# Second layer's u and z weights: the unrounded rest made by an adding transfer in place of a VectorE subtraction

## Chip, core and metric

The kernel runs on one core of one Trainium2 chip. The time is that of one execution on the device in microseconds; what is compared is the median of several executions. The core has five engines that work side by side, each through its own queue of instructions in order: TensorE (PE, the matmuls, with PEld for the loading of weights), VectorE (DVE), ScalarE (ACT), GpSimd (POOL) and SyncE (SP, which issues transfers). Sixteen DMA engines carry the transfers that these queues issue.

## What is computed

A trunk of two layers is applied to 512 prompt tokens and to 8 samples of 4 tokens (544 tokens in all), with a width of 1024. The first layer is an RWKV-7 mixer, the second a gated MLP over chunks of 128 tokens. The change lies in the second:

```python
def _gmlp_mixer(h, w_in, v_g, v_b, ws, bs, w_out):
    proj = h @ w_in                       # 1024 -> 3 x 2048
    u = jax.nn.gelu(proj[..., :e])
    v = jax.nn.gelu(proj[..., e:2 * e])
    z = proj[..., 2 * e:]
    ...                                   # v is normalised
    mixed = jnp.einsum('gts,bcsgd->bctgd', wm, vp) + bs.T[None, None, :, :, None]
    ...
    o = u * mixed * jax.nn.silu(z)
    return o @ w_out, v
```

All inputs and outputs are float32.

## The kernel before

**Precision.** PE multiplies in a rounded float32 format (float32r in the code). To keep the product close to float32, each operand is split in two: a rounded part (`hi`) and the rest that rounding dropped (`lo` = raw - hi). One product then takes three matmuls: `mm3` (L218 to L221) runs hi weights with hi activations (L219), hi weights with lo activations (L220), and lo weights with hi activations (L221), in this order. So every block of weights needs two further steps between its load and its use.

**Weights.** `load` (L117) takes a slot of the tag "raw" and has SP issue the transfer of a block from memory: 128 partitions x 1024 values, 512 KB. `halves` (L122) rounds it on ACT into a slot of "whi" (L125) and has DVE subtract the rounded from the raw block into a slot of "wlo" (L126). `weights` (L129) does one after the other. Each of the three tags has two slots, shared by all weights of the kernel: a block takes the slot of the block before last, and may write to it only when that one's last reader is done.

**The second layer's loop** (L1401 to L1429) goes over f = 0 to 15, 128 columns of u and z at a time. In each turn `project` (L230) is called for u (L1409; the names in the profile are gu_r for the raw block, gu_h and gu_l for its parts, gu_p for the result) and for z (L1425; gz_r, gz_h, gz_l, gz_p). A call makes the two parts of the weights, then runs two halves of 272 tokens of 8 x 3 matmuls each, 48 in all, and evacuates each half from the result bank: DVE multiplies by the norm's factor (L1406, L1420) and ACT takes the Gelu (L1407) or the Tanh (L1422). Between the two calls stands `mix(f - 1)` for f > 0 (L1376): ten small matmuls (L1382, L1383), then DVE and ACT form the gated output of the block and split it (goh, gol). Results rotate over five PSUM banks (`bank`, L225).

After f = 4, 8 and 12, `out_project` (L238) multiplies four finished blocks by the output weights: eight small blocks of weights (go_r, go_h, go_l; 256 KB each) with 24 matmuls each (go__p), which take their slots from the same three tags, and DVE adds the results to the residual xT (L247). At f = 12 the residual is also transposed (L1446, pfy; L1452 and L1453 for the samples, with two copies on POOL). In the tail behind the loop (L1455 to L1558) the last four blocks are multiplied out, added and normed.

In this loop nobody writes the order of the instructions by hand. A planner takes the program and lays out each engine's queue ahead of time, by the order of the program and by its own estimates of when operands and slots are ready; it also places all semaphores. The queues are then fixed, and each engine runs its own in order. (The first layer's order is written out by hand; it isn't touched. Nor are the v weights of the second layer or its output weights, which keep `halves`.)

Of the kernel before, what the change touches and what calls it, by code (L numbers as in the profile page):

```python
# [7 lines left out]
F32R = mybir.dt.float32r  # L8
ALU = mybir.AluOpType
AF = mybir.ActivationFunctionType  # L10
# [5 lines left out]
KD = 8  # L16
# [58 lines left out]
def build(tc, A, O, off):  # L75
    nc = tc.nc
    V, S, G, T, Q = nc.vector, nc.scalar, nc.gpsimd, nc.tensor, nc.sync
# [3 lines left out]
    with ctx:  # L81
        cp = ctx.enter_context(tc.tile_pool(name="cp", bufs=1))
        wp = ctx.enter_context(tc.tile_pool(name="wp", bufs=3))
# [33 lines left out]
        def load(name, src, nk, w=128, q=Q):  # L117
            raw = wp.tile([128, 1024 // w, w], F32, name=name + "_r", tag="raw", bufs=2)
            q.dma_start(raw[:, 0:nk, :], src)
            return name, raw, nk, w  # L120

        def halves(name, raw, nk, w=128):  # L122
            hi = wp.tile([128, 1024 // w, w], F32R, name=name + "_h", tag="whi", bufs=2)
            lo = wp.tile([128, 1024 // w, w], F32R, name=name + "_l", tag="wlo", bufs=2)
            S.activation(hi[:, 0:nk, :], raw[:, 0:nk, :], AF.Copy)  # L125
            V.tensor_tensor(out=lo[:, 0:nk, :], in0=raw[:, 0:nk, :], in1=hi[:, 0:nk, :], op=ALU.subtract)  # L126
            return hi, lo

        def weights(name, src, nk, w=128):  # L129
            return halves(*load(name, src, nk, w))  # L130
# [6 lines left out]
        with tc.tile_pool(name="st", bufs=1) as st:  # L137
# [46 lines left out]
            for h in range(2):  # L184
                for k in range(KD):
                    ks = slice(128 * k, 128 * k + 128)
                    pool, tag = banks[(8 * h + k) % 6]
# [30 lines left out]
        def mm3(ps, whi, wlo, ahi, alo, first, last):  # L218
            T.matmul(ps, whi, ahi, start=first, stop=False)  # L219
            T.matmul(ps, whi, alo, start=False, stop=False)  # L220
            T.matmul(ps, wlo, ahi, start=False, stop=last)  # L221
# [3 lines left out]
        def bank(name):  # L225
            pool, tag = ((ppp, "pp"), (ppp, "pp"), (p1, "g"), (p1, "s"), (p1, "y"))[turn_[0] % 5]
            turn_[0] += 1
            return pool.tile([128, 512], F32, name=name, tag=tag)

        def project(name, w, evac):  # L230
            hi, lo = weights(name, w, KD)
            for h in range(2):
                ps = bank(name + "_p")[:, 0:HT]
                for k in range(KD):
                    mm3(ps, hi[:, k, :], lo[:, k, :], hh[:, k, h, :], hl[:, k, h, :], k == 0, k == KD - 1)
                evac(h, ps)
# [997 lines left out]
        with tc.tile_pool(name="l1", bufs=1) as l1, tc.tile_pool(name="l1t", bufs=2) as lt:  # L1234
# [166 lines left out]
            for f in range(NF):  # L1401
                gu = lt.tile([128, 2, HT], F32, name=f"gu{f}", tag="gu", bufs=2)

                def uevac(h, ps, f=f, gu=gu):
                    a = lt.tile([128, HT], F32, name=f"ua{f}", tag="va")
                    V.tensor_tensor(out=a, in0=ps, in1=bc[:, h, :], op=ALU.mult)  # L1406
                    S.activation(gu[:, h, :], a, AF.Gelu_apprx_tanh)  # L1407

                project(f"gu{f}", A["g_u"][f], uevac)  # L1409
                if f % 4 == 0:  # L1410
                    normalise(f // 4)
# [6 lines left out]
                def z1evac(h, ps, f=f, gz=gz):  # L1418
# [4 lines left out]
                    V.scalar_tensor_tensor(out=gz[:, h, :], in0=th, scalar=1.0, in1=a, op0=ALU.add, op1=ALU.mult)  # L1423

                project(f"gz{f}", A["g_z"][f], z1evac)  # L1425
                V.scalar_tensor_tensor(out=gz, in0=gu, scalar=0.5, in1=gz, op0=ALU.mult, op1=ALU.mult)
                if f in (4, 8, 12):
# [40 lines left out]
            for q in range(4):  # L1468
                if q < 2:
                    hi, lo = (wp.tile([128, 4, 256], F32R, name=f"gl{q}_{n}", tag=f"w{n}", bufs=2) for n in ("hi", "lo"))  # L1470
                else:
                    hi, lo = (x[:, :, 256 * q - 512 : 256 * q - 256] for x in (hv, lv))
                raw = ws[:, :, 256 * q : 256 * q + 256]
# [137 lines left out]
```

## Time and profile before

| | |
|---|---|
| time, median of 3 runs | 1267.81 us (1265.22 to 1268.55) |
| the profiled execution's own time | 1269.8 us |
| its span, first to last instruction | 1268.0 us |
| mean granted TensorE clock | 0.998 |
| the u and z loop in the span | from 948.5 to about 1241 us |
| the same: u matmuls (gu_p), per line L219, L220, L221 | 256 each |
| loads gu_r and gz_r | 16 each, 512 KB, issued by SP |

The profile is of one execution. A row of a group reads: line, engine, operation, output<-input, partitions x elements, count | busy us in all, mean ns of one | us for which the engine stood idle just before them, and what ended that idle time. In a timeline a row begins with its start (us from the start of the span) and its duration. Matmuls overlap in the pipeline, so the starts of two that follow each other are closer (0.12 to 0.13 us) than the duration shown (0.29 us). SPq marks the issue of a transfer by SP.

### The profile page before, as it was taken

The page shows a single profiled execution, that of the slowest core. Times are in us where ns is not written, and L with a number is a line of the kernel's source. Part 1 is how long each engine was busy: PE and PEld are TensorE (multiplying, and loading weights), DVE is VectorE, ACT ScalarE, POOL GpSimd, SP SyncE. Part 2 cuts the span into 40 slices and gives each one's busy share as a digit, 9 for nine tenths or more (in the row PEclk, how much of TensorE's full clock was granted, in tenths as well). Part 3 has the DMA queues.
Part 4 walks back from the last instruction along what each step waited for, and adds up shares of the span by engine and source line. Part 5 has one row for each costly group of instructions (what it writes and reads, how often), then busy time and mean ns, then how long its engine had stood idle before and what let it go on. Part 6 is the DMA issues. An engine that isn't in the chain of part 4 may idle for free.

```text
span 1268.0 us, 34549 instructions
## 1 busy us (share of the span) xinstructions
PE 1229.7 (97%) x14432; PEld 1154.6 (91%) x14432; DVE 949.8 (75%) x2205; ACT 663.0 (52%) x1523; POOL 132.4 (10%) x346
## 2 busy tenths in 40 slices
PE   6999999999999999999998999999999999999997
PEld 5899999999999999999997889987779999999997
DVE  5789999999999999998987866573248656656466
ACT  5677567657666775676665552243243323232343
POOL 1212021111102120211211100100000000000000
PEclk9999999999999999999999999999999999999999
DMA  5322432332333234224232363432222232231511
GB/s 179 100 73 82 112 88 76 103 94 73 91 103 92 64 86 119 66 77 116 68 89 71 106 193 113 140 98 70 98 94 77 64 110 79 78 103 58 164 37 71
DMA packets 113508, 119.74 MB, mean 94 GB/s; under 512 B 77992, under 2 KB 81448, under 8 KB 113352
## 3 DMA queue, kind: packets, MB, share of 16 engines
q1 hardware_dynamic: 113352, 117.54, 30.8%
q8 instruction: 113, 1.85, 0.6%
q14 instruction: 43, 0.35, 0.1%
HBM read 99.79 MB, written 17.72 MB: 93 GB/s over the span
## 4 chain that ended last, share of the span: by engine, by line
PE 85%; DVE 6%; DMA 4%; ACT 3%; issue 1%; POOL 1%; SPq 1%; POOLq 0%; DVEq 0%; ACTq 0%
PE r_p L219 3%; PE gz_p L219 3%; PE v_p L219 3%; PE gu_p L219 3%; PE gz_p L220 3%; PE gz_p L221 3%; PE gu_p L221 3%; PE gu_p L220 3%; PE k_p L219 2%; PE r_p L221 2%; PE r_p L220 2%; PE gv_p L1317 2%; PE pgo L547 2%; PE v_p L221 2%; PE v_p L220 2%; PE gv_p L1318 2%
## 5 line engine op out<-in xcount | busy, mean ns | idle before, releaser
L219 PE MATMUL v_p<-hh,v_h 128*128 128x272 f32 x256 | 78.6, 307 | 0.9 <-ACT raw L362 0.9
L219 PE MATMUL r_p<-hh,r_h 128*128 128x272 f32 x256 | 78.8, 308 | 0.0
L219 PE MATMUL k_p<-hh,k_h 128*128 128x272 f32 x256 | 78.3, 306 | 0.0
L219 PE MATMUL z_p<-hh,z_h 128*128 128x272 f32 x256 | 77.7, 304 | 0.0
L219 PE MATMUL gz_p<-hh,gz_h 128*128 128x272 f32 x256 | 75.2, 294 | 0.0
L221 PE MATMUL r_p<-hh,r_l 128*128 128x272 f32 x256 | 74.2, 290 | 0.0
L219 PE MATMUL gu_p<-hh,gu_h 128*128 128x272 f32 x256 | 74.2, 290 | 0.0
L220 PE MATMUL r_p<-hl,r_h 128*128 128x272 f32 x256 | 74.1, 289 | 0.0
L221 PE MATMUL gu_p<-hh,gu_l 128*128 128x272 f32 x256 | 73.9, 289 | 0.0
L220 PE MATMUL gu_p<-hl,gu_h 128*128 128x272 f32 x256 | 73.9, 289 | 0.0
L221 PE MATMUL z_p<-hh,z_l 128*128 128x272 f32 x256 | 73.8, 288 | 0.0
L221 PE MATMUL gz_p<-hh,gz_l 128*128 128x272 f32 x256 | 73.8, 288 | 0.0
L221 PE MATMUL k_p<-hh,k_l 128*128 128x272 f32 x256 | 73.8, 288 | 0.0
L221 PE MATMUL v_p<-hh,v_l 128*128 128x272 f32 x256 | 73.8, 288 | 0.0
L220 PE MATMUL gz_p<-hl,gz_h 128*128 128x272 f32 x256 | 73.7, 288 | 0.0
L220 PE MATMUL k_p<-hl,k_h 128*128 128x272 f32 x256 | 73.7, 288 | 0.0
L220 PE MATMUL v_p<-hl,v_h 128*128 128x272 f32 x256 | 73.6, 288 | 0.0
L220 PE MATMUL z_p<-hl,z_h 128*128 128x272 f32 x256 | 73.6, 287 | 0.0
L221 PE MATMUL go__p<-goh,go_l 128*128 128x272 f32 x192 | 55.5, 289 | 0.0
L219 PE MATMUL go__p<-goh,go_h 128*128 128x272 f32 x192 | 55.3, 288 | 0.0
L220 PE MATMUL go__p<-gol,go_h 128*128 128x272 f32 x192 | 55.1, 287 | 0.0
L364 POOL COPY shl<-raw 128x9 f32<-128x9 f32 x49 | 11.0, 225 | 409.6 <-ACT raw L362 409.4
(415 smaller groups left out, 4487.9 us busy)
## 6 DMA issues: line engine op xcount, KB each, us to landing
k_r<-w_in SPq DMA_DIRECT2D x16, 512.0 KB
r_r<-w_in SPq DMA_DIRECT2D x16, 512.0 KB
v_r<-w_in SPq DMA_DIRECT2D x16, 512.0 KB
z_r<-w_in SPq DMA_DIRECT2D x16, 512.0 KB
gu_r<-g_u SPq DMA_DIRECT2D x16, 512.0 KB
gz_r<-g_z SPq DMA_DIRECT2D x16, 512.0 KB
go_r<-g_out SPq DMA_DIRECT2D x24, 256.0 KB
od<-of SPq DMA_DIRECT2D x16, 272.0 KB
```

What stands on the lines that cost most here:

```text
L219: T.matmul(ps, whi, ahi, start=first, stop=False)
L220: T.matmul(ps, whi, alo, start=False, stop=False)
L221: T.matmul(ps, wlo, ahi, start=False, stop=last)
L364: G.tensor_copy(shl[:, :, f], raw[:, 512:553:5])
L547: T.matmul(pg[h][:, 128 * j : 128 * j + 128], BK[rs, c].rearrange("p a b -> p (a b)"), AR[rs, :, c, :], start=True, stop=True)
L1317: T.matmul(ps[i], ah, hi, start=k == 0, stop=False)
L1318: T.matmul(ps[i], al, hi, start=False, stop=False)
```

## The change

`project` no longer calls `weights`. It loads the raw block as before and rounds it on ACT as before. The lo tile is then first filled with the negated rounded block, by a second pass on ACT (a copy with scale -1). After that POOL issues a transfer that reads the same block of weights from memory a second time and adds it, in the DMA engines, onto what stands in the tile: lo = -hi + w. The subtraction on DVE goes away, for the 32 blocks of u and z. `halves`, `out_project`, the v weights and the first layer stay.

```diff
         def project(name, w, evac):
-            hi, lo = weights(name, w, KD)
+            _, raw, nk, _ = load(name, w, KD)
+            hi = wp.tile([128, KD, 128], F32R, name=name + "_h", tag="whi", bufs=2)
+            lo = wp.tile([128, KD, 128], F32R, name=name + "_l", tag="wlo", bufs=2)
+            S.activation(hi, raw, AF.Copy)
+            S.activation(lo, hi, AF.Copy, scale=-1.0)
+            G.dma_start(lo, w, accum_op=ALU.add)
             for h in range(2):
                 ps = bank(name + "_p")[:, 0:HT]
                 for k in range(KD):
```

## The prediction

> **What bounds the kernel now.** I read the page's busy shares first, then its DMA queues, then the busy time by stretches for the second layer's u and z loop (from the first u matmul at 948.5 to the last z matmul, about 1241) and for the tail behind it.
>
> ```profile
> PE 1229.7 (97%) x14432; PEld 1154.6 (91%) x14432; DVE 949.8 (75%) x2205; ACT 663.0 (52%) x1523; POOL 132.4 (10%) x346
> ...
> q1 hardware_dynamic: 113352, 117.54, 30.8%
> q8 instruction: 113, 1.85, 0.6%
> q14 instruction: 43, 0.35, 0.1%
> ...
> 948.50:1241.00 292.50, 292.44 (x2346) 291.55 (x2347) 185.65 (x372) 91.73 (x152) 2.01 (x4) 1.00 0.27 86
> 1241.00:1268.00 27.00, 20.35 (x188) 19.07 (x186) 14.99 (x45) 11.13 (x40) 2.73 (x5) 0.95 0.21 83
> ```
>
> The columns of the stretches are PE, PEld, DVE, ACT and POOL busy, then granted clock, DMA share and GB/s. In the loop PE is busy 292.44 of 292.50 us at full clock; DVE has 107 us to spare, ACT 201, POOL almost everything. So the loop is a row of matmuls with nothing between them, and whatever VectorE is spared there can give back at most 0.06 us. The change can only cost, unless it reaches the 6.65 us without PE in the tail, where no u or z weight is made. No queue of POOL's appears among the DMA queues: what the change adds has no row of its own in this trace.
>
> Next I looked at how early the weights are ready, in groups by line and shape (count, busy us, mean ns, idle before and its releaser).
>
> ```profile
> L126 DVE TENSOR_TENSOR gz_l<-gz_r,gz_h 128x1024 fp32r<-128x1024 f32 x16 | 19.6, 1225 | 11.1 <-ACT gz_h L125 11.0
> L126 DVE TENSOR_TENSOR gu_l<-gu_r,gu_h 128x1024 fp32r<-128x1024 f32 x16 | 19.5, 1216 | 4.6 <-ACT gu_h L125 4.6
> L125 ACT ACTIVATE gz_h<-gz_r 128x1024 fp32r<-128x1024 f32 x16 | 17.0, 1061 | 32.5 <-PE gz_p L220 21.9 <-PE go__p L220 5.9 <-DMA gz_r<-g_z 4.8
> L125 ACT ACTIVATE gu_h<-gu_r 128x1024 fp32r<-128x1024 f32 x16 | 16.9, 1057 | 28.4 <-PE gu_p L220 18.0 <-PE go__p L220 7.1 <-DMA gu_r<-g_u 3.2
> ```
>
> The rounding on ACT is mostly released by PE (gu_p, gz_p, go__p L220): with two slots for rounded weights, block n+1 can be rounded only when PE has finished block n-1, that is while block n runs. The weights themselves have long landed. So what counts is the time from the end of block n-1 to the first matmul of block n+1 that reads the rest (L221).
>
> **The change part by part.** Removed: 32 subtractions on DVE, 19.6 + 19.5 = 39.1 us. DVE isn't the bound, so this gives nothing by itself, and what becomes late in its place is the new chain. Added on ACT: 32 negations of the same shape as the rounding, 1.06 us each, about 34 us on an engine with 201 us free. A Gelu or Tanh behind one waits up to 1.06 us longer; it is hidden by the block of 48 matmuls (about 6 us, from 954.66 to 960.81 in the rows below) that PE runs meanwhile, since the result banks rotate by five. Added on POOL: 32 transfers of 512 KB, which wait there for the negation. Behind them in POOL's queue stand only the next transfers and, after the last output block, two small copies for PE's transposes. SP's loads are freed earlier:
>
> ```profile
> SPq L119 <- DVE gu_l L126: 71.7, 12, 7.7
> ```
>
> This is the loads' own wait for the subtraction; it now ends with the rounding. That gains nothing, as ACT waited for loads for only 3.2 + 4.8 us in all, at the start of the loop.
>
> The path that can set the end is rounding, negation, transfer, first L221. Call X the time from the end of the negation to the matmul being free to go. Four places have different room for X.
>
> ```profile
> 1000.23 1.06 ACT L125 ACTIVATE gz_h<-gz_r 128x1024 fp32r<-128x1024 f32 x1 [1.99 <-PE gz_p L220]
> 1007.50 0.29 PE L221 MATMUL gz_p<-hh,gz_l 128*128 128x272 f32 x1
> ...
> 954.66 1.06 ACT L125 ACTIVATE gu_h<-gu_r 128x1024 fp32r<-128x1024 f32 x1
> 960.81 0.29 PE L221 MATMUL gu_p<-hh,gu_l 128*128 128x272 f32 x1
> ...
> 1034.44 1.06 ACT L125 ACTIVATE gu_h<-gu_r 128x1024 fp32r<-128x1024 f32 x1 [2.38 <-PE go__p L220]
> 1037.63 0.29 PE L221 MATMUL gu_p<-hh,gu_l 128*128 128x272 f32 x1
> ...
> 1188.07 1.06 ACT L125 ACTIVATE gu_h<-gu_r 128x1024 fp32r<-128x1024 f32 x1 [2.38 <-PE go__p L220]
> 1192.48 0.28 PE L221 MATMUL gu_p<-hh,gu_l 128*128 128x272 f32 x1
> ```
>
> These are rows in order of time (start, duration). After two ACT passes (2.12 us) the room is:
> - in the steady pattern 1007.50 - 1000.23 - 2.12 = 5.15 us. If block gu(f) is late by d, gz(f) behind it gains that d, so a late chain costs X - 5.15 once in each f, not twice. It holds for f = 2, 3, 4, 6, 7, 8, 10, 11, 12, 14, 15: 11 times.
> - at gu1, where no mix stands between gu0 and gz0: 960.81 - 954.66 - 2.12 = 4.03 us, once.
> - at gu5 and gu9, behind the output projection whose blocks last only some 3 us: 1037.63 - 1034.44 - 2.12 = 1.07 us, twice. Today's subtraction needs 1.2 us there from the end of the rounding and just fits.
> - at gu13: 1192.48 - 1188.07 - 2.12 = 2.29 us; the transposes pfy that stand among its matmuls could be moved ahead by the planner, which I don't count on.
>
> So the cost is 11(X - 5.15) + (X - 4.03) + 2(X - 1.07) + (X - 2.29), each bracket only where positive; above 5.15 it is 15X - 65.1.
>
> Now X, bounded by rows.
>
> ```profile
> 935.70 0.33 SPq L119 DMA_DIRECT2D gu_r<-g_u  x1
> 939.08 1.06 ACT L125 ACTIVATE gu_h<-gu_r 128x1024 fp32r<-128x1024 f32 x1 [3.15 <-DMA gu_r<-g_u]
> ...
> 1037.50:1040.00 2.50, 2.50 (x22) 2.50 (x21) 1.66 (x2) 1.02 (x1) 0.00 (x0) 1.00 0.61 210
> ...
> 951.51 1.19 POOL L1353 TENSOR_TENSOR rl<-rl,nhalf 128x5 f32<-128x5 f32 x1
> ...
> DMA packets 1028, 0.06 MB, mean 65 GB/s; under 512 B 1028, under 2 KB 1028, under 8 KB 1028
> ...
> 371.00:372.00 1.00, 1.00 (x10) 1.00 (x10) 0.93 (x4) 0.64 (x2) 0.00 (x0) 1.00 0.64 65
> ```
>
> A plain load of 512 KB on SP's queue took 939.08 - 935.70 = 3.38 us from issue to the rounding that waited for it: the low end, as the new transfer moves these bytes too. Its data kept all 16 DMA engines busy for 2.5 x 0.61 = 1.5 us (the second stretch holds one such load, 210 GB/s x 2.5 us = 0.52 MB). Adding must also read the target, so I take the data twice: +1.5 us. POOL issues it in place of SP; for its setup I take the dearest POOL instruction of the stage, 1.2 us, though it may be nothing. X = 3.4 + 1.5 + 1.2 = 6.1 us. The far end is a transfer cut into small pieces: the stretch 371 to 372 moved 0.065 MB in 0.64 us of all engines, so 2 x 0.52 MB would need 10.3 us, and X = 3.4 - 1.5 + 10.3 + 1.2 = 13.4 us. I take 6.1, nearest to the load's own rows, since the tile is laid out as in that load.
>
> Sum at X = 6.1: 15 x 6.1 - 65.1 = 26.4 us (10.5 steady, 2.1 at gu1, 10.1 at gu5 and gu9, 3.8 at gu13). Memory traffic doesn't add to this: 32 x 3 us in 292 us lifts the DMA share from 0.27 to about 0.6. The profiled execution took 1269.8 us, of which 1268.0 are its span; it becomes 1296.2. The median shown is 1267.8, 2.0 below, so I forecast 1294.
>
> The Trainium skill, DMA: Bandwidth & Descriptors, section "Anatomy of one DMA", gives a POOL-issued transfer as 2.0 us plus bytes over 436 GB/s; for 512 KB this is an estimate of 3.2 us, by which the sum would be 5.2 us and the time 1273. No run here shows a POOL transfer; the plain load above, at 3.38 us, lies close. Against the change speaks SBUF — State Buffer, section "Who interferes with whom" of the Trainium skill: while VectorE runs in a mode that takes both ports, POOL cannot write its descriptors.
>
> ```profile
> L1358 DVE TENSOR_SCALAR Vt<-Vt,mv,rl 128x512 f32<-128x512 f32 x16 | 8.0, 531 | 1.7 <-POOL rl L1353 1.7
> ```
>
> This is the loop's candidate, at 1.04 ns per column against 1.19 for the subtractions above. That isn't the halving such a mode would show, so by this trace the lock should add nothing; held up by one such instruction, a transfer would lose at most 0.53 us.
>
> **The rivals.**
> - Light transfer: X between 3.4 and 5.15, setup hidden or the target read alongside. Steady blocks don't wait; the places behind the output projection do: 5.8 us at 3.4, 12.1 at 5.15, so 1274 to 1280. For it: the load's 3.38 us. Against: the extra read. Chance 0.27. The formula of the Trainium skill falls here.
> - Heavy transfer: X from 7.5 to 13.4, because adding is slower than reading, or POOL prepares slowly. 47 to 136 us, so 1315 to 1404. For it: small packets do run at 65 GB/s here. Against: whole rows of 4 KB are contiguous. Chance 0.24.
> - Not slower (the other side): the planner orders everything in this loop anew. If it lets gu5, gu9 and gu13 be rounded one output block (3 us) earlier, their room grows to 4.1 to 5.3 us, and with X below 4.03 no place waits: 1268. For it: it already mixes gu13 with the transposes. Against: slots are given out in the order of the program, and PE's idle 0.06 us leaves nothing to win. Chance 0.06.
> - It doesn't do what it says: a rounded target may make the transfer go element by element. At 0.64 x 16 / 1028 = 10 ns a packet, 2 x 131072 elements on 16 engines need 164 us per transfer, and the loop becomes milliseconds. Chance 0.05.
>
> **How the numbers follow.** The forecast case, X from 5.15 to 7.5 (1280 to 1315), has 0.38. The range must leave out no more than 2 in 10: I drop the element-wise case, most of the not-slower case, and the heavy one above X = 10 (15 x 10 - 65.1 = 85 us, 1353), about 0.09. That gives 1272 to 1353. A measurement of this kernel can tell about 0.3% (3.8 us) from no change. Even the lightest transfer costs 5.8 us, so "within" is nearly all of the not-slower case: faster 0.02, same 0.05, slower 0.93.
>
> **What would show it.** POOL's queue with 32 issues; PE idle before gu_p L221 and gz_p L221, put down to a transfer. X read as the gap from the end of a negation to that matmul; PE waits of about X - 1.07 at gu5 and gu9, and of X - 5.15 once in each steady f. DVE 39 us lighter, ACT 34 us heavier. The forecast is wrong if steady blocks don't wait (X under 5.15), if both blocks of each f wait (then the slots aren't what links them), or if ACT's rounding starts late for another reason.

## The result and the profile after

| | before | after |
|---|---|---|
| median (lowest to highest) of 4 runs each | 1268.18 us (1265.22 to 1273.35) | 1305.8 us (1299.48 to 1311.6) |
| the profiled execution, its span | 1269.8, 1268.0 us | 1311.6, 1309.8 us |

The changed kernel takes 1.0291 times as long, with an interval of 1.0261 to 1.0321: 37.6 us more, where 26 were forecast. The profile is of one of the longer executions, 41.8 us longer in its span, and that is the number to be explained.

First the page of after: busy time by engine, and two of the DMA queues (packets, MB, share of 16 engines).

```profile
PE 1242.3 (95%) x14432; PEld 1165.4 (89%) x14432; DVE 917.0 (70%) x2173; ACT 693.3 (53%) x1555; POOL 160.6 (12%) x378
...
q1 hardware_dynamic: 113352, 117.54, 29.8%
q0 software_dynamic: 4608, 16.78, 7.7%
```

The work moved as the diff says. DVE lost 32 instructions and 32.8 us, ACT gained 32 and 30.3 us, POOL gained 32 and 28.2 us, and a queue that wasn't there before carries 16.78 MB, which is 32 blocks of 512 KB. (Busy time counts overlapping records once; the durations of the instructions that went and came add up to 39.1 us on DVE and 33.5 on ACT.) PE has the same 14432 matmuls but is busy 12.6 us longer. So the same matmuls took it longer, and that was no part of the forecast.

The busy time by stretches, the loop and then the tail (columns as in the prediction):

```profile
948.10:1282.70 334.60, 306.51 (x2350) 302.60 (x2347) 154.49 (x342) 120.53 (x183) 28.21 (x34) 0.96 0.53 122
1282.70:1309.80 27.10, 20.40 (x188) 19.13 (x187) 15.04 (x45) 11.13 (x40) 2.75 (x5) 0.97 0.21 83
```

All of it is in the loop: 334.6 us where it was 292.5, while the tail kept its 27 us. PE now stands idle for 334.60 - 306.51 = 28.1 us there and is busy for 306.51 - 292.44 = 14.1 us more (over the whole kernel it is 12.6, since outside the loop PE's busy time also differs between the two executions), and its granted clock is 0.96 where it was 1.00. The list of PE's waits (us in total, times, longest) names the releaser:

```profile
PE gu_p L221 <- DMA gu_l<-g_u: 26.8, 14, 3.5
...
PE gz_p L221 <- DMA gz_l<-g_z: 1.3, 2, 1.0
```

These two rows make 28.1 us. So 41.8 = 28.1 of waiting for the adding transfers + 12.6 by which PE is busy longer + about 1 elsewhere.

One chain, at f = 6, in the timeline of after (start, duration, engine, and in brackets the idle time before it):

```profile
1059.48 1.06 ACT L234 ACTIVATE gu_h<-gu_r 128x1024 fp32r<-128x1024 f32 x1 [1.75 <-PE gu_p L220]
1060.77 1.05 ACT L235 ACTIVATE gu_l<-gu_h 128x1024 fp32r<-128x1024 f32 x1
1062.11 0.86 POOL L236 DMA_DIRECT2D gu_l<-g_u  x1 [10.25 <-ACT gu_l L235]
...
1065.20 0.29 PE L219 MATMUL gu_p<-hh,gu_h 128*128 128x272 f32 x1
1067.48 0.39 PE L221 MATMUL gu_p<-hh,gu_l 128*128 128x272 f32 x1 [2.00 <-DMA gu_l<-g_u]
```

It is the chain that the prediction drew: PE's last use of an old slot releases the rounding, then come negation, POOL's issue, the landing, and the first L221. X, from the end of the negation (1061.82) to L221, is 5.66 us here. The matmul before L221 started at 1065.20, and matmuls follow each other by 0.125 us, so PE was ready for L221 at 1065.33. The room was 3.5 us, and PE stood idle for about the rest.

### The profile page after: what moved, and what is told of

The parts are those of the page before. It is cut to its first block, busy times and chain, and to the rows that moved or that the text cites. A ratio compares the mean times of both kernels' runs of the same rounds, so it can differ in the third digit from the quotient of the medians.

```text
span 1309.8 us, 34637 instructions
## 1 busy us (share of the span) xinstructions
PE 1242.3 (95%) x14432; PEld 1165.4 (89%) x14432; DVE 917.0 (70%) x2173; ACT 693.3 (53%) x1555; POOL 160.6 (12%) x378
## 3 DMA queue, kind: packets, MB, share of 16 engines
q0 software_dynamic: 4608, 16.78, 7.7%
## 5 line engine op out<-in xcount | busy, mean ns | idle before, releaser
L221 PE MATMUL gu_p<-hh,gu_l 128*128 128x272 f32 x256 | 79.0, 311 | 26.8 <-DMA gu_l<-g_u 26.8
L221 PEld LDWEIGHTS gu_p<-hh,gu_l 128*128 128x128 f32 x256 | 52.2, 205 | 29.8 <-DMA gu_l<-g_u 29.8
L219 PE MATMUL gu_p<-hh,gu_h 128*128 128x272 f32 x256 | 78.0, 306 | 0.0
L220 PE MATMUL gu_p<-hl,gu_h 128*128 128x272 f32 x256 | 77.8, 304 | 0.0
L1411 DVE TENSOR_TENSOR ua<-gu_p,bc 128x272 f32<-128x272 f32 x32 | 14.1, 441 | 90.1 <-PE gu_p L221 90.1
L221 PE MATMUL gz_p<-hh,gz_l 128*128 128x272 f32 x256 | 73.7, 289 | 1.3 <-DMA gz_l<-g_z 1.3
L221 PE MATMUL r_p<-hh,r_l 128*128 128x272 f32 x256 | 74.4, 291 | 0.0
L220 PE MATMUL r_p<-hl,r_h 128*128 128x272 f32 x256 | 74.4, 291 | 0.0
L221 PE MATMUL z_p<-hh,z_l 128*128 128x272 f32 x256 | 73.9, 288 | 0.0
L221 PE MATMUL k_p<-hh,k_l 128*128 128x272 f32 x256 | 73.8, 288 | 0.0
L221 PE MATMUL v_p<-hh,v_l 128*128 128x272 f32 x256 | 73.7, 288 | 0.0
L220 PE MATMUL k_p<-hl,k_h 128*128 128x272 f32 x256 | 73.7, 288 | 0.0
L220 PE MATMUL v_p<-hl,v_h 128*128 128x272 f32 x256 | 73.7, 288 | 0.0
L220 PE MATMUL gz_p<-hl,gz_h 128*128 128x272 f32 x256 | 73.6, 288 | 0.0
L220 PE MATMUL z_p<-hl,z_h 128*128 128x272 f32 x256 | 73.6, 287 | 0.0
L953 POOL TENSOR_TENSOR m<-m,nhalf 128x9 f32<-128x9 f32 x16 | 34.3, 2144 | 177.9 <-DVE m L951 177.9
```

The lines of the kernel that those rows point to most:

```text
L953: G.tensor_tensor(out=m2, in0=m2, in1=nhalf[:, 0:9], op=ALU.pow)
```

## The experiments

Two theories stood against each other. **Theory A**, of the prediction: a block costs what its chain (rounding, negation, transfer) lacks in room before the first L221, so a late chain is paid once per f and goes away with room. **Rival B**: the 32 transfers, ACT passes or POOL issues cost by themselves (traffic, queues, contention), so each costs its share wherever its result is used. Then it had to be found out where the 12.6 us of PE's busy time came from. Each ratio is against the kernel before on the same chip; its medians there were 1267.15 us (19 runs) for `u_only`, `z_only`, `idle_transfers` and `rest_last`, 1269.73 (11) for `third_slot`, `neg_first`, `plain` and `warm`, and 1269.13 (14) for `rest_later_2`, `halves` and `again`.

**Only the u blocks, only the z blocks.** `u_only` and `z_only` use the new chain for one of the two and the old subtraction for the other (the diff is that of `u_only`; `z_only` asks for "gz"):

```diff
-            _, raw, nk, _ = load(name, w, KD)
...
+            if name.startswith("gu"):
+                _, raw, nk, _ = load(name, w, KD)
...
+                G.dma_start(lo, w, accum_op=ALU.add)
+            else:
+                hi, lo = weights(name, w, KD)
```

> The new chain for the u weights alone; z keeps VectorE's subtraction. Theory A (a late chain costs PE once in each f, since a wait at gu gives gz its room; long waits then halve the granted clock for some us): nearly the whole loss stays, 1298 to 1308 us against 1268 before and 1306 with both; PE waits before gu_p L221 of about 27 us. Rival B (each of the 32 transfers costs its own share of the 38 us): half, 1287 us.

Measured: 1299.58 us, ratio 1.0259 (1.0221 to 1.0297), within A's range.

> The new chain for the z weights alone; u keeps VectorE's subtraction. Theory A: the steady blocks wait once in each f, now before gz_p L221, some 1.5 us in 12 turns, but not behind the output projection, where gz has 3 us more room: 15 to 20 us of waits and a little clock, 1283 to 1293 us; so the two halves together lose clearly more than the whole. Rival B: the halves add up to the whole, with u_only at 1287 this one at 1287.

Measured: 1301.53 us, ratio 1.0271 (1.0233 to 1.031), longer than either theory gave. The list of PE's waits in `u_only` has for the loop:

```profile
PE gu_p L221 <- DMA gu_l<-g_u: 22.8, 15, 3.6
```

And that of `z_only`:

```profile
PE gz_p L221 <- DMA gz_l<-g_z: 19.2, 15, 2.6
```

The changed kernel keeps its 26.8 us of u waits nearly whole when the z blocks are taken out of the change (22.8), and its two z waits become 15 when the u blocks are. Either half costs 32 to 34 us; both together cost 38, not 67. A price per transfer is ruled out by that; that it is paid once per f stands. What made `z_only` longer than expected isn't the waiting (19.2 us, where theory A had 15 to 20) but PE's busy time, 1243.3 us, 13.6 above before, 11.0 of it in the loop (297.81 us from the first u to the last z matmul, 286.83 before). Theory A had allowed for only "a little clock" there.

**The transfers without a waiter.** `idle_transfers` is the kernel before plus, for each block, a transfer of 512 KB that adds onto a spare tile which nobody reads, released by the rounding:

```diff
             hi, lo = weights(name, w, KD)
+            G.tensor_copy(sc[:, 0, 0:1], hi[:, 0, 0:1])
+            G.dma_start(sc, w, accum_op=ALU.add)
```

> The kernel before, VectorE's subtraction kept, and beside it 32 adding transfers of the same blocks into a spare tile that nobody reads, each released by the rounding of its block through a copy of one column on POOL. Theory A: 1267 to 1271 us, no PE waits. Rival C: if the transfers' traffic or POOL's issues disturb the others, 1280 us or more.

Measured: 1269.05 us, ratio 1.0011 (0.9994 to 1.0028). Its loop:

```profile
948.50:1241.00 292.50, 292.44 (x2356) 291.35 (x2349) 185.73 (x373) 92.16 (x153) 40.60 (x66) 1.00 0.59 142
```

PE is busy 292.44 of 292.50 us, exactly as before, though the DMA share went from 0.27 to 0.59. Traffic and POOL's queue cost nothing; B falls for these.

**The same chain, used later.** `rest_last` keeps the whole change (32 negations, 32 adding transfers) and only turns the order of the 48 matmuls: those on `hi` of both halves first, the 16 on the rest last. That puts 32 matmuls between the start of a block and its first use of `lo`.

```diff
+            pss = [bank(name + "_p")[:, 0:HT] for _ in range(2)]
             for h in range(2):
-                ps = bank(name + "_p")[:, 0:HT]
                 for k in range(KD):
-                    mm3(ps, hi[:, k, :], lo[:, k, :], hh[:, k, h, :], hl[:, k, h, :], k == 0, k == KD - 1)
-                evac(h, ps)
+                    T.matmul(pss[h], hi[:, k, :], hh[:, k, h, :], start=k == 0, stop=False)
+                    T.matmul(pss[h], hi[:, k, :], hl[:, k, h, :], start=False, stop=False)
+            for h in range(2):
+                for k in range(KD):
+                    T.matmul(pss[h], lo[:, k, :], hh[:, k, h, :], start=False, stop=k == KD - 1)
+                evac(h, pss[h])
```

> The change as it is, but PE runs the 32 matmuls of a block that read the rounded weights first, for both halves, and the 16 that read the rest last: the need for the rest moves 4 us later, and the rounding comes out of its chain. All transfers and both passes on ACT stay. Theory A: room grows from 5.15 to some 10 us, and to some 6 behind the output projection; PE waits nearly vanish, granted clock 1.00, 1268 to 1273 us. Rival C (the loss comes from the transfers' traffic, from ACT's 34 us or from POOL): no cover helps, 1290 us or more.

Measured: 1269.19 us, ratio 1.0011 (0.9988 to 1.0035). Its engines on the page:

```profile
PE 1227.0 (97%) x14432; PEld 1153.0 (91%) x14432; DVE 916.4 (72%) x2173; ACT 695.7 (55%) x1555; POOL 159.8 (13%) x378
```

And its loop among the stretches:

```profile
948.50:1241.00 292.50, 289.67 (x2328) 288.54 (x2327) 151.27 (x334) 122.02 (x179) 27.84 (x33) 1.00 0.58 138
```

DVE, ACT and POOL show the changed kernel's work, yet PE is idle for 2.8 us instead of 28.1 (two waits, at gu5 and gu9), the clock is back at 1.00, and no difference from before can be told. The ACT passes are excluded with that too. The 37 us are the price of waiting in the wrong place, with what a wait costs PE besides, and not of the work itself.

**In between.** `rest_later_2` does the same within each half: 16 matmuls on `hi`, then 8 on `lo`.

```diff
                 for k in range(KD):
-                    mm3(ps, hi[:, k, :], lo[:, k, :], hh[:, k, h, :], hl[:, k, h, :], k == 0, k == KD - 1)
+                    T.matmul(ps, hi[:, k, :], hh[:, k, h, :], start=k == 0, stop=False)
+                    T.matmul(ps, hi[:, k, :], hl[:, k, h, :], start=False, stop=False)
+                for k in range(KD):
+                    T.matmul(ps, lo[:, k, :], hh[:, k, h, :], start=False, stop=k == KD - 1)
```

> The change with the matmuls on the rest moved last within each half of a block: the first need comes 2 us later (16 matmuls), half of the move in rest_last, and the rounding's slot comes free 1 us before the block's end. Theory A: room for the transfer grows from 5.15 to some 8 us, steady waits vanish; gu1, gu5, gu9 and gu13 keep up to 2 us each: 1270 to 1278 us, PE waits under 8 us. If the cover were not what counts, about 1300.

Measured: 1276.42 us, ratio 1.0075 (1.0046 to 1.0105). Its waits:

```profile
PE gu_p L243 <- DMA gu_l<-g_u: 5.3, 2, 3.0
```

Two waits are left, at gu5 and gu9 behind the output projection (3.0 and 2.3 us); all others are covered. Behind the first the clock was halved for 3.4 us, behind the second it wasn't, as the stretches behind the two show:

```profile
1041.10:1044.40 3.30, 3.30 (x17) 3.30 (x16) 0.44 (x1) 0.43 (x1) 0.00 (x0) 0.50 0.92 202
1121.40:1124.40 3.00, 3.00 (x24) 3.00 (x25) 0.44 (x1) 0.83 (x2) 0.00 (x0) 1.00 1.01 209
```

**An earlier start by a third slot.** In `third_slot` every third block has a `lo` tile of its own, so that the chain of a block needn't wait for the block before last. For this the tile is filled ahead of `hi`, with the negated raw block; the write rounds it as it rounds `hi`, so the sum is the same.

```diff
-                lo = wp.tile([128, KD, 128], F32R, name=name + "_l", tag="wlo", bufs=2)
-            S.activation(hi, raw, AF.Copy)
-            S.activation(lo, hi, AF.Copy, scale=-1.0)
+            if n % 3 == 2:
+                lo = uzp.tile([128, KD, 128], F32R, name=name + "_l", tag="uzl", bufs=1)
+            else:
+                lo = wp.tile([128, KD, 128], F32R, name=name + "_l", tag="wlo", bufs=2)
+            S.activation(lo, raw, AF.Copy, scale=-1.0)
             G.dma_start(lo, w, accum_op=ALU.add)
+            S.activation(hi, raw, AF.Copy)
```

> A third slot for the rest (every third block of u and z takes it), and the negation made straight from the raw block, so that negation and transfer of block n+1 can start one block earlier. The same bytes, passes and transfers. Theory A (the loss is the chain from the end of block n-1): room grows by about 6 us, no waits but perhaps behind the output projection, 1268 to 1272 us. If the chain's start isn't what counts (the transfer is late for another reason), it stays at 1290 us or more.

Measured: 1285.97 us, ratio 1.0134 (1.0106 to 1.0162): more than half of the loss is gone, but far more is left than was expected. Its waits in the loop:

```profile
PE gu_p L221 <- DMA gu_l<-g_u: 9.8, 3, 3.8
...
PE gu_p L219 <- ACT Vt L1332: 1.8, 1, 1.8
```

Every steady wait is gone, as A has it. The three left are at gu5, gu9 and gu13. There the slot is held by the blocks of the output projection, or, at gu13, the chain waits for the raw block itself (the row of ACT there):

```profile
1201.44 1.06 ACT L237 ACTIVATE gu_l<-gu_r 128x1024 fp32r<-128x1024 f32 x1 [2.05 <-DMA gu_r<-g_u]
```

The expectation had only a "perhaps" for these places: gu5 and gu9 get no third slot of their own (their n, 10 and 18, leaves the remainders 1 and 0), and at gu13, which has it, the raw block comes late. Moving the first pass also cost 1.8 us at the start of the loop, where ACT's v blocks (Vt) now come later, and PE was busy 7.0 us longer.

**The negation first, the rest a little later.** `neg_first` fills `lo` before `hi` is made (as the last one, without the extra tile), and moves the last L220 of a half behind its last L221.

```diff
-            S.activation(hi, raw, AF.Copy)
-            S.activation(lo, hi, AF.Copy, scale=-1.0)
+            S.activation(lo, raw, AF.Copy, scale=-1.0)
             G.dma_start(lo, w, accum_op=ALU.add)
+            S.activation(hi, raw, AF.Copy)
...
+                T.matmul(ps, hi[:, KD - 1, :], hl[:, KD - 1, h, :], start=False, stop=True)
```

> The negation made from the raw block ahead of the rounding, and the last of the matmuls on the rest moved ahead of the last on the rounded weights, so that its slot comes free first. The chain loses one pass on ACT, 1.06 + 0.23 us; bytes and transfers stay. Theory A: 11 steady waits and most of the halved clock go, 1276 to 1288 us. Rival (the transfer's end is set by the memory traffic, not by its start): within 5 us of 1306.

Measured: 1296.21 us, ratio 1.0206 (1.0178 to 1.0234), above the expected range. Its waits:

```profile
PE gu_p L243 <- DMA gu_l<-g_u: 13.7, 8, 3.2
...
PE gu_p L240 <- ACT Vt L1333: 2.1, 1, 2.1
```

The steady waits fell to at most 0.9 us each, as a chain that starts one ACT pass earlier should give. But gu1, gu5, gu9 and gu13 kept 2.8 to 3.2 us each (at the last three the planner still put the rounding first), there were 2.1 us at the start of the loop, and PE was busy 7.1 us longer. Only the steady places had been counted.

**The adding alone.** `plain` writes the tile with a transfer of the same size that doesn't add.

```diff
-            G.dma_start(lo, w, accum_op=ALU.add)
+            G.dma_start(lo, w)
```

> The transfer on POOL without adding: it overwrites the negated block, so the output lacks the subtraction of the rounded part. Theory A: a packet of 4 KB takes 159 ns as in a plain load in place of 328, the transfer is shorter by 8 x 0.17 = 1.35 us; steady waits nearly vanish, gu1, gu5, gu9 and gu13 still wait 1 to 2.5 us: 1273 to 1284 us. Rival (adding costs nothing, POOL's path does): no change from 1300 to 1306 us.

Measured: 1284.29 us, ratio 1.0133 (1.01 to 1.0167), just above its range. POOL's issues (duration in ns: least, median, most) and the time from issue to landing, in the view of the tile gu_l of after:

```profile
L236 POOL DMA_DIRECT2D gu_l<-g_u x16: 860/862/1172, 941.3 to 1258.5; - x16
...
DMA to landing us min/median/max: 5.3/5.7/7.7
```

The same view of `plain`:

```profile
L236 POOL DMA_DIRECT2D gu_l<-g_u x16: 527/528/1170, 940.2 to 1229.9; - x16
...
DMA to landing us min/median/max: 3.7/4.5/5.5
```

Adding lengthens the landing by 1.2 us at the median, of which 0.33 us are POOL's issue. The PE waits fell to 11.8 us and PE was busy 1230.7 us. Even the plain transfer from POOL took 4.5 us, more than the 3.38 us of the plain load on SP from issue to its reader. The Trainium skill, DMA: Bandwidth & Descriptors, section "Anatomy of one DMA", with its 2.0 us plus bytes over 436 GB/s (3.2 us here, an estimate), is too short for both.

**Two smaller transfers.** `halves` cuts the transfer in two of 256 KB each.

```diff
-            G.dma_start(lo, w, accum_op=ALU.add)
+            for b in range(2):
+                G.dma_start(lo[:, 4 * b : 4 * b + 4], w[:, 4 * b : 4 * b + 4], accum_op=ALU.add)
```

> The change with the transfer in two of 256 KB (columns k 0 to 3, then 4 to 7), both issued by POOL one behind the other; the first matmul on the rest waits for the first alone. If a transfer's time is mostly its bytes, the first lands some 1.4 us earlier, steady waits nearly vanish, 1284 to 1294 us. If it is mostly a fixed part (issue, start, landing), little changes, 1297 to 1304 us.

Measured: 1296.98 us, ratio 1.0212 (1.0174 to 1.025), at the border between the two. POOL's issues of gu_l:

```profile
L237 POOL DMA_DIRECT2D gu_l<-g_u x32: 856/1120/1242, 942.2 to 1243.8; - x32
```

Half the bytes don't have a shorter issue (0.86 us at the least, 1.12 at the median, against 0.86 for the whole). At the eight blocks where PE waited for the first half, that came 4.6 to 5.8 us after the end of the negation, 5.1 at the mean, where the whole block takes 6.3 in after: half the bytes are worth some 1.2 us, near the 1.4 of the first theory. But the second half lands about 2 us behind the first, so that PE waits twice in four blocks (gu1, gu5, gu9 and gu10), and PE is busy 1239.0 us. By that some 3.9 of the 6.3 us don't go with the bytes (an estimate); what they consist of wasn't tried.

**Does the slow clock follow the waits?** `warm` gives PE 16 matmuls more, whose results are overwritten, at the head of nine blocks that wait (gu1, gu5 to gu11, gu13): 18 us more work, put into the waits.

```diff
+                if h == 0 and name in ("gu1", "gu5", "gu6", "gu7", "gu8", "gu9", "gu10", "gu11", "gu13"):
+                    for j in range(16):
+                        T.matmul(ps, hi[:, j % KD, :], hh[:, j % KD, h, :], start=True, stop=True)
```

> The change as it is, with 16 more matmuls (2.0 us of PE) at the head of the nine u blocks that waited 1.6 us or more; their result is overwritten. 18 us more work for PE, all in time in which it waited. If the granted clock halves because PE stood idle, the waits shrink to at most 2 us, the clock stays at 1.00, and the kernel is faster for doing more: 1291 to 1299 us. If the clock has nothing to do with the waits: 1303 to 1310 us.

Measured: 1304.56 us, ratio 1.0282 (1.0253 to 1.031). The time stands with the second theory, the profile with the first: the waits are 10.7 us (but the longest is 2.9, over the 2 expected) and PE is busy 1251.7 us, which is 1229.7 of before, 18 of added work and 4 more, where after had 12.6. In the record of the granted clock it falls to 0.50 twice in this loop, at the two waits that are left over 2 us (2.8 at gu5, 2.9 at gu9); at the other seven blocks it stays full. That agrees with the clock following idleness, but the part lost differs from run to run, so this run alone doesn't settle it.

**The same kernel again.** `again` is the changed kernel, nothing altered, for a second trace to compare places with.

> The changed kernel once more, unaltered, for a second profile and more times: does the part lost to the halved clock differ from one execution to the next? If the clock's gate samples time on its own grid, waits of 2 to 3 us hit it in one execution and miss it in another: PE waits again 26 to 30 us, but PE busy anywhere from 1234 to 1243 us and times from 1297 to 1312 us. If the clock follows each wait in the same way, PE busy 1242 us again and the same blocks slow.

Measured: 1308.2 us, ratio 1.0308 (1.0278 to 1.0338).

```profile
PE gu_p L221 <- DMA gu_l<-g_u: 22.7, 13, 3.4
PE gz_p L221 <- DMA gz_l<-g_z: 3.6, 3, 2.1
```

26.3 us of waits, and PE is busy 1238.2 us, 8.5 above before. Now the stretches of 3 us right behind two waits in after (at gu1 and gu5):

```profile
964.20:967.20 3.00, 3.00 (x13) 3.00 (x14) 0.85 (x2) 0.16 (x1) 0.86 (x1) 0.50 0.61 142
1053.70:1056.70 3.00, 2.93 (x23) 2.93 (x24) 0.00 (x0) 0.00 (x0) 0.00 (x0) 1.00 1.00 224
```

And behind those at gu5 and gu9 in `again`:

```profile
1055.00:1058.00 3.00, 2.94 (x13) 2.94 (x14) 0.00 (x0) 0.00 (x0) 0.00 (x0) 0.50 1.02 231
1141.80:1144.80 3.00, 2.96 (x23) 2.96 (x24) 0.00 (x0) 0.00 (x0) 0.00 (x0) 1.00 1.04 213
```

In 3 us PE does 23 matmuls at clock 1.00 and 13 at 0.50. Right behind a wait the clock is often halved, but not always: in after the wait at gu5 left it full and that at gu9 halved it, in `again` the other way round, with waits of 2.4 to 2.7 us each time.

What decides it can be read from the record of the granted clock. In the loop of after it stands at 0.50 from 963.55, 1083.02, 1144.46, 1175.18 and 1233.21 us, each time for 3.41 us or for 6.83; and these starts lie 35, 18, 9 and 17 times 3.413 us apart, on one grid. Two steps of that grid around the wait at gu5 in after, and two around that at gu9:

```profile
1048.89:1052.30 3.41, 2.52 (x22) 2.33 (x21) 2.37 (x7) 2.06 (x3) 0.86 (x1) 1.00 0.88 189
1052.30:1055.71 3.41, 1.94 (x15) 1.94 (x16) 0.73 (x1) 0.37 (x1) 0.00 (x0) 1.00 0.97 241
...
1141.05:1144.46 3.41, 0.82 (x7) 0.63 (x7) 1.83 (x4) 0.66 (x1) 0.75 (x1) 1.00 1.01 234
1144.46:1147.87 3.41, 3.41 (x17) 3.41 (x17) 0.00 (x0) 0.00 (x0) 0.00 (x0) 0.50 0.86 177
```

A border of the grid cuts the wait at gu5 in two, 0.89 us idle in one step and 1.47 in the next, and the clock stays full; that at gu9 lies whole in one step (2.59 us idle), and the next step is at half clock. It is the same in the loops of all the traces: each of the 27 steps at full clock in which PE was idle for 1.79 us or more was followed by one at 0.50, of the six with 1.70 to 1.75 us two were, and none with less. So about half a step of idle time is enough, and which wait is hit depends on where the grid happens to lie. At gu1 it stayed halved for two steps, 6 us of which are behind the wait; the last slow and the first full matmuls in after:

```profile
970.00 0.43 PE L219 MATMUL gu_p<-hh,gu_h 128*128 128x272 f32 x1
970.22 0.36 PE L220 MATMUL gu_p<-hl,gu_h 128*128 128x272 f32 x1
970.43 0.29 PE L221 MATMUL gu_p<-hh,gu_l 128*128 128x272 f32 x1
970.55 0.29 PE L219 MATMUL gu_p<-hh,gu_h 128*128 128x272 f32 x1
```

Their starts are 0.22 us apart while the clock is halved and 0.12 after. From 964.16 to 970.22 that is some 27 matmuls at 0.1 us too much, 2.7 us for one wait.

## Why the prediction held, and where its terms were off

The sign, the mechanism, the place and X were right; the sizes of four terms were off, and one term was missing. That the waits together came within 2 us of the forecast is luck, as the four errors nearly cancel (+1.4, -5.1, -0.9 and +6.3 us). The room at each place is read as in the rows at gu6: from the end of the negation to the start of the last matmul before L221, plus 0.125 us.

| term of the sum | forecast | in the trace of after |
|---|---|---|
| X | 6.1 us | 5.7 to 8.0, mean 6.3 (14 u blocks that wait, each read as at gu6) |
| gu1 | 2.1 | 3.5 |
| gu5 + gu9 | 10.1 | 5.0 |
| gu13 | 3.8 | 2.9 |
| steady turns | 10.5 | 16.8 |
| waits together | 26.4 | 28.1 |
| PE busy longer in the loop | none | 14.1, some 10 of it at half clock |

**X.** The three parts (a plain load, the target read as well, POOL's setup) held as a sum: a plain transfer from POOL takes 4.5 us where load and setup were put at 3.4 + 1.2, and the adding 1.2 us where 1.5 was put; the 0.3 us between the end of the negation and POOL's issue make up for it. The 1.2 us for the setup, the duration of another POOL instruction, fitted by luck: POOL's issue measures 0.86 us, and 0.53 without adding.

**gu5, gu9 and the steady turns** have one cause: the planner moved work. PE's rows before L221 of gu5 in after:

```profile
1048.97 1.05 PE L1387 MATMUL pmx<-wst,Vt 128*128 128x128 f32 x8
1049.86 0.31 PE L1388 MATMUL pms<-wsx,Vs 128*128 128x32 f32 x2
1050.01 0.37 PE L219 MATMUL gz_p<-hh,gz_h 128*128 128x272 f32 x1
...
1050.59 0.83 PE L1387 MATMUL pmx<-wst,Vt 128*128 128x128 f32 x6
1053.77 0.39 PE L221 MATMUL gu_p<-hh,gu_l 128*128 128x272 f32 x1 [2.36 <-DMA gu_l<-g_u]
```

The whole mix of f - 1, four matmuls of gz5 and six of the eight pmx of the next mix stand there, from 1048.97 to 1051.27: 2.3 us of work that the program has later. The negation ended at 1047.69, so the room is 3.6 us instead of 1.07, and the wait 2.36 us instead of 5.0. But this work is missing in the rooms behind it. At f = 6 the room is 3.5 us (first section). At f = 7 only the two pmx that were left stand in between:

```profile
1073.22 0.38 PE L1387 MATMUL pmx<-wst,Vt 128*128 128x128 f32 x2
...
1074.59 1.05 ACT L235 ACTIVATE gu_l<-gu_h 128x1024 fp32r<-128x1024 f32 x1
...
1079.82 0.29 PE L220 MATMUL gu_p<-hl,gu_h 128*128 128x272 f32 x1
1083.63 0.59 PE L221 MATMUL gu_p<-hh,gu_l 128*128 128x272 f32 x1 [3.53 <-DMA gu_l<-g_u]
```

The room is 1079.95 - 1075.64 = 4.3 us, where it is 5.0 in the turns with nothing moved (f = 2, 3, 8, 12, 14, 15). The same stands at f = 10 and 11. These four turns waited 2.00 + 3.53 + 2.14 + 2.03 = 9.7 us, where the forecast had 4 x 0.95 = 3.8; the other seven waited 7.05 us, where it had 6.65. So the steady formula fits where nothing was moved (room 5.0 against 5.15), and most of the 5 us saved at gu5 and gu9 were paid in the next two turns. The prediction had named this freedom of the planner for gu13 (where the room was 3.6 us in place of 2.29) and for the rival alone. At f = 7 there is more: X is 8.0 us here and 6.2 in `again`. Why a transfer lands late at times wasn't tried.

**gu1.** The formula let the two ACT passes follow each other. In the timeline of after a Gelu stands between them:

```profile
954.32 1.07 ACT L234 ACTIVATE gu_h<-gu_r 128x1024 fp32r<-128x1024 f32 x1
956.93 0.43 ACT L1412 ACTIVATE gu<-ua 128x272 f32<-128x272 f32 x1 [1.54 <-DVE ua L1411]
957.27 1.04 ACT L235 ACTIVATE gu_l<-gu_h 128x1024 fp32r<-128x1024 f32 x1
```

The negation starts 957.27 - 955.39 = 1.9 us after the rounding's end, because ACT's queue has the Gelu first, and that waited for DVE. The room fell from 4.03 to 2.2 us. The prediction had asked how long a Gelu waits behind a negation, and not how long the negation waits behind a Gelu.

**Busy longer.** Nothing in the trace of before could show it, since PE never waited in the loop; but a forecast of 28 us of waits needs a sentence on what PE does after one. It is the missing term: 14.1 us in the loop beside 28.1 of waits in after. It has two parts. In after the clock stood at 0.50 for 23.9 us of the loop, and PE worked in 22.7 of them, that is some 100 matmuls at 0.1 us too much, about 10 us (an estimate). The rest comes with each wait even at full clock: `plain`, where the clock stayed at 1.00 through the loop, was busy 288.91 us from the first u to the last z matmul, where before was 286.83, so 2.1 us for its 8 waits. The duration of a matmul (0.29 us, and 0.39 for the first one after a wait, as in the rows at gu6) shows in full at a wait, and is otherwise covered by the next one. For the 16 waits of after that makes about 4 us. In `again` the clock was halved for only 6.8 us of the loop, and PE was busy 294.26 us there, 7.4 above before: some 3 from the clock and some 4 from the 16 waits. The Trainium skill, TensorE: Matmul & The Clock Gate, section "Part 1: The HAM clock gate (the "warmup" mystery)", has the rule: the clock halves after a window of about 3.4 us without work, free-running, and is full again after a busy one. The grid of 3.413 us and gu5 and gu9 changing places between two traces agree with that; that a whole window must be idle doesn't, as 2.59 us of one at gu9 in after were enough, and 2.03 us before the spell at 1175.18.

**VectorE's lock.** The prediction read TENSOR_SCALAR's 1.04 ns per column as no doubled rate. But a duration has a fixed part, as a second row of before shows:

```profile
L1390 DVE TENSOR_TENSOR mx<-mx,gz 128x544 f32<-128x544 f32 x16 | 11.5, 719 | 0.1
```

With the subtractions' 1216 ns for 1024 columns this makes about 1.04 ns per column and 0.16 us besides, by which 512 columns would take 0.69 us (an estimate, if TENSOR_SCALAR runs at the same rate); the TENSOR_SCALAR took 0.53. So the trace of before didn't rule the lock out.

**What the prediction said would show.** 32 issues on POOL: yes. DVE 39 us lighter and ACT 34 heavier: 32.8 and 30.3. Waits put down to a transfer, once per f: yes, with the z blocks waiting only twice (1.3 us), so "both blocks wait" didn't come. Waits of X - 1.07 at gu5 and gu9: no, 2.4 and 2.6 us, by the planner's doing above. Traffic adds nothing: shown by `idle_transfers`.

**The rivals.** Light transfer: no, the steady turns wait. Heavy: no, X stays near 6. Not slower: no; the room that it needs behind the output projection (over 4.1) wasn't there (3.6), with X at 6 in any case. Element by element: no, the transfer lands after 5.7 us.

## What to carry to other kernels

When a step is moved from an idle engine to a path with a longer latency, its cost isn't the engine's share but the room between the release of its slot and the first use of its result: count this for each place of a loop, and for what a planner moves in between. Where the room is short, first look for a later place of the first use: the order of the matmuls alone took this change from 38 us to no difference, while an extra slot took it only halfway. And price a wait of PE above its length: here each cost some 0.25 us more at full clock, and one that filled about half a step of the clock's grid cost 1.6 to 3 us more at half clock.

## What the hardware showed that I hadn't expected

- PE's clock goes by a grid of 3.413 us that is fixed within an execution: in these loops a step at 0.50 followed each step in which PE had been idle for 1.79 us or more, and none with less than 1.70. At gu1 the half clock lasted two steps (2.7 us lost). The same wait can be hit in one execution and missed in another.
- A transfer that adds takes POOL 0.86 us to issue, where one of the same size that only writes takes 0.53 us, and each half of it, in two transfers, doesn't take less (0.86 us at the least, 1.12 at the median).
- POOL's issue for gu1, 0.86 us elsewhere in the loop, took 1.17 us in after and 1.52 in `neg_first`, where VectorE ran its normalising TENSOR_SCALARs beside it:

```profile
954.66 1.44 DVE L1367 TENSOR_SCALAR Vt<-Vt,mv,rl 128x512 f32<-128x512 f32 x3
955.09 1.52 POOL L235 DMA_DIRECT2D gu_l<-g_u  x1 [3.10 <-ACT gu_l L234]
```

The Trainium skill, SBUF — State Buffer, section "Who interferes with whom", lets an instruction of VectorE that takes both ports hold up POOL's descriptors, and counts TENSOR_SCALAR among the candidates. The prediction gave this nothing, with at most 0.53 us an instruction. The 0.3 and 0.7 us seen at this place (0.6 in `plain`, 1.17 us beside 0.53) agree with the rule, but the two weren't tried apart, and in after gu0's issue took 1.06 us with VectorE idle.
